# Own places for the decay matrices of a delta rule, and unread products in a matmul engine's gaps

## The chip, the cores and the metric

The kernel runs on one core of one Trainium2 chip. The metric is device time in microseconds of one execution of the whole program. A core has a matmul engine (PE), three engines for elementwise work (DVE, ACT and POOL) and a queue engine (SP) that only issues transfers; each works its own instructions in a fixed order, and semaphores join them. The profile shows for every stretch of time the clock that PE was granted, as a share of full speed.

## The reference

One layer of a diffusion backbone with post-norm, over 512 latent tokens and 256 context tokens of width 1024, all in float32. Cut to what matters here:

```python
# half-step SwiGLU FFN (d_ff 2816) with adaLN shift/scale/gate from c, then in parallel
#   neighbourhood attention (8 heads of 64) and a gated DeltaNet (4 heads of 128, both
#   directions), merged by sigmoid gates, then a second half-step SwiGLU FFN.
def gated_delta_chunks(q, k, v, g, beta, s0, with_output):   # chunks of 64 tokens
    g      = cumsum(g)                                       # within a chunk
    decay  = exp(where(lower, g[..., :, None] - g[..., None, :], -inf))
    m      = where(strict, (k * beta) @ k.T * decay, 0)
    u, w   = solve(eye + m, [v * beta, k * beta * exp(g)])   # unit lower triangular
    # over the chunks: v_new = u - w S;  S = S * exp(g_end) + k_tail.T v_new
    #                  o = (q exp(g)) S + (q @ k.T * decay) v_new

def branch_merge(o_a, o_b, gate_a, gate_b, w_pa, w_pb, w_o):
    y = sigmoid(gate_a) * (o_a @ w_pa) + sigmoid(gate_b) * (o_b @ w_pb)
    return y @ w_o
```

## The kernel before

**Products.** A float32 operand is split into a high part, which ACT casts (`split`, L135), and a low part, which DVE subtracts from the source (L137). Every product of a weight is then three matmuls, high by high, low by high and high by low (`mm3k`, L190 to L192). A weight of 128x1024 comes by DMA into `wr`, is split into `wh` and `wl`, and serves 8 tiles of 128 rows. `uxh` and `uxl` are the parts of the modulated latent tokens, `uch` and `ucl` those of the context tokens.

**Stages.** First come the modulation vectors (`w_ada`, L279 on DVE) with the first FFN's up products (to 213 us), then its down products with the layer norms (to 610 us). Then the projections of `w_in` follow, and with them the delta rule's preparation (to 745 us), the delta rule itself, laid between the rest of those projections (to 993 us), attention in four head pairs with the delta rule's output gates between them (to 1093 us), the merge with `w_pa` (to 1119 us) and `w_o` (to 1140 us). The second FFN begins with up products over half the tokens, goes on with units of seven products (1200 to 1400 us), and ends with its down products and the last norm.

**The delta rule.** It works in three groups of four "grams". A gram is one pair of heads p and one step s, with four 64-token chunk matrices side by side (two heads, two directions; 128x4x128). For each (`gram`, L914) SP loads the row of cumulated decays spread over all partitions into `Dt` (L918, 256 KB, from `gcd`); DVE subtracts the column and adds the mask (L921, four instructions); ACT takes the exponential; DVE multiplies it by the key products into `Bt` (L927, four instructions); SP writes `Bt` to DRAM (`bd`, L928); and where queries are due, DVE multiplies `Dt` with the query products into `At` (L931). `Dt` is a ring of two places: a third load waits until a gram has read its own decays for the last time.

`base_inverse` (L935) reads a group's `bd` back as 32x32 blocks (`L`, `Ltr`, L947), solves all of them by 31 steps of a multiply and a sum on DVE (L954, L955), and writes the result to DRAM (`rd`, L959). `inverse` reads it as `T` (L976), and PE joins the blocks (L857, `pi`). Between these instructions PE works off the rest of the projections (`fills`; their results leave PSUM by ACT into `spill`, L609). While group 0's base inverse runs on DVE, group 1's grams run between its steps; group 0's `inverse` cannot begin before its base inverse has ended.

**Order.** The program is written once, and a planner with a model of each engine's time sets every engine's order. `tc.issue_after(x)` binds an instruction behind instruction `x` in that plan. Tiles come from rings by tag and count, so a tag's next tile waits for the release of the one that many places before.

**Attention.** For a head pair, `att_load` (L1163) brings query, key and context key (`qa`, `ka`, `kc`), ACT casts their high parts (L1169) and POOL subtracts the low parts in place (L1170). `attend` computes scores for four blocks (L1240), exponentials on ACT (L1248), a scaling by the row sum on POOL (L1251), transposes on PE (L1255), the copy of the transposed block to SBUF on ACT (`pT`, L1257) and the products with the values (`po`, L1266).

## Time and profile before

| What | Value |
|---|---|
| Time of three runs | 1526.37, 1526.87 and 1531.96 us; median 1526.87 us |
| The profiled execution | 1530.66 us; its span 1528.8 us |
| Mean granted clock | 0.988 |
| PE busy | 1462.6 us of the span |
| DVE, ACT, POOL busy | 1050.0, 605.4, 226.8 us |

The profiled execution is one of its own, 3.79 us above the median of the three. Its span leaves out 1.86 us that its time has. A row of a timeline gives an instruction's start and length, its engine and line, what it writes and reads, and in square brackets the idle time ahead of it with what ended it; PE's lengths overlap, since matmuls are pipelined, so that the distance from one start to the next is the pace. A row of windows gives each engine's busy time in a stretch, then the granted clock, the DMA share and the rate.

### The profile page before, as it was taken

To read this page: it belongs to the slowest core of one execution; us is meant where nothing else is said; L and a number is where in the kernel's file an instruction comes from. 1 tells how busy PE (TensorE), PEld (TensorE's weight loads), DVE (VectorE), ACT (ScalarE), POOL (GpSimd) and SP (SyncE) were. 2 spreads that over 40 slices of the span, in tenths; PEclk is the share of its full clock that TensorE was granted. 3 is DMA by queue.
4 is the path that set the end of the run, shared out by engine and by line. 5 is a ranking of instruction groups with operands and counts; after the bars stand their busy time and mean duration, and the time that the engine had idled before them with its cause. 6 is when DMAs were issued, how large, how long until landed. Compare 5 with 4: busy or idle time off the path is not lost.

```text
span 1528.8 us, 23646 instructions
## 1 busy us (share of the span) xinstructions
PE 1462.6 (96%) x9221; PEld 1258.7 (82%) x9221; DVE 1050.0 (69%) x1792; ACT 605.4 (40%) x1005; POOL 226.8 (15%) x224
## 2 busy tenths in 40 slices
PE   6999999999999999999996899999999999999997
PEld 4779988888888887889875778867678999998886
DVE  8765942597554587768777895576669699886426
ACT  5444221322222255546543444266416444344310
POOL 0000000000000011323301001366421022220001
PEclk9999999999999999999998999999999999999999
DMA  9665742667454334222476634283353143333422
GB/s 370 207 237 180 222 142 97 211 213 260 168 192 146 130 112 137 87 90 79 141 216 180 172 99 122 69 284 117 91 174 138 56 139 102 106 110 139 138 83 83
DMA packets 107586, 230.72 MB, mean 151 GB/s; under 512 B 34177, under 2 KB 47825, under 8 KB 107473
## 3 DMA queue, kind: packets, MB, share of 16 engines
q1 hardware_dynamic: 105312, 221.79, 44.7%
q10 hardware_dynamic: 1586, 5.32, 0.9%
q0 software_dynamic: 576, 2.10, 0.4%
q8 instruction: 72, 1.18, 0.3%
q14 instruction: 40, 0.33, 0.1%
HBM read 206.33 MB, written 22.85 MB: 150 GB/s over the span
## 4 chain that ended last, share of the span: by engine, by line
PE 76%; DVE 10%; DMA 7%; issue 3%; ACT 2%; POOL 2%; SPq 0%; DVEq 0%; ACTq 0%; POOLq 0%
PE ps L209 19%; PE ps L190 8%; PE ps L192 8%; PE ps L191 8%; PE pm L190 5%; PE pm L192 5%; PE pm L191 5%; PE pc L857 2%; PE ps L1478 2%; PE ps L1480 2%; PE ps L1479 2%; DVE wl L137 2%; PE po L1266 1%; DMA T<-rd 1%; PE pt L1255 1%
## 5 line engine op out<-in xcount | busy, mean ns | idle before, releaser
L137 DVE TENSOR_TENSOR wl<-wr,wh 128x1024 fp32r<-128x1024 f32 (+1 forms) x215 | 263.0, 1228 | 195.1 <-ACT wh L135 194.3
L135 ACT CAST wh<-wr 128x1024 fp32r<-128x1024 f32 (+1 forms) x215 | 217.8, 1018 | 333.4 <-PE ps L209 105.0
L192 PE MATMUL ps<-uxh,wl 128*128 128x512 f32 (+1 forms) x496 | 179.6, 363 | 2.2 <-DVE wl L137 2.2
L191 PE MATMUL ps<-uxl,wh 128*128 128x512 f32 (+1 forms) x496 | 179.3, 363 | 0.8 <-DVE uxl L137 0.8
L190 PE MATMUL ps<-uxh,wh 128*128 128x512 f32 (+1 forms) x496 | 179.6, 365 | 0.0
L279 DVE SCALAR_TENSOR_TENSOR adap<-wr,crow 128x1024 f32<-128x1024 f32 x112 | 136.8, 1221 | 38.5 <-DMA wr<-in_w_adaT_dram 37.1
L112 POOL TENSOR_TENSOR rs<-ve,mhalf 128x1 f32<-128x1 f32 (+2 forms) x46 | 50.4, 1099 | 744.6 <-DVE ve L108 735.4
L190 PE MATMUL pm<-uxh,wh 128*128 128x512 f32 x320 | 133.0, 416 | 4.1 <-ACT spill L609 2.1
L192 PE MATMUL pm<-uxh,wl 128*128 128x512 f32 x320 | 128.2, 401 | 0.7 <-DVE wl L137 0.7
L191 PE MATMUL pm<-uxl,wh 128*128 128x512 f32 x320 | 127.8, 399 | 0.0
L192 PEld LDWEIGHTS ps<-uxh,wl 128*128 128x128 f32 x496 | 93.7, 189 | 17.9 <-DVE wl L137 3.3
L191 PEld LDWEIGHTS ps<-uxl,wh 128*128 128x128 f32 x496 | 94.0, 189 | 14.9 <-DVE uxl L137 1.0
L190 PEld LDWEIGHTS ps<-uxh,wh 128*128 128x128 f32 x496 | 93.4, 189 | 14.3 <-issue 0.8
L190 PE MATMUL ps<-uch,wh 128*128 128x256 f32 x352 | 98.6, 280 | 0.0
L192 PE MATMUL ps<-uch,wl 128*128 128x256 f32 x352 | 98.3, 279 | 0.0
L191 PE MATMUL ps<-ucl,wh 128*128 128x256 f32 x352 | 98.2, 279 | 0.0
L209 PE MATMUL ps<-wh,hx 128*128 128x512 f32 x352 | 94.8, 389 | 0.0
L209 PEld LDWEIGHTS ps<-wh,hx 128*128 128x128 f32 x352 | 65.9, 188 | 13.6
L190 PEld LDWEIGHTS pm<-uxh,wh 128*128 128x128 f32 x320 | 61.6, 193 | 16.3 <-ACT spill L609 3.0
L192 PEld LDWEIGHTS pm<-uxh,wl 128*128 128x128 f32 x320 | 61.7, 193 | 14.8 <-DVE wl L137 1.5
L191 PEld LDWEIGHTS pm<-uxl,wh 128*128 128x128 f32 x320 | 61.6, 192 | 10.6
L190 PEld LDWEIGHTS ps<-uch,wh 128*128 128x128 f32 x352 | 66.1, 188 | 0.6
(411 smaller groups left out, 3438.7 us busy)
## 6 DMA issues: line engine op xcount, KB each, us to landing
wr<-in_w_adaT_dram SPq DMA_DIRECT2D x88, 512.0 KB, 4.7
wr<-in_up_dram SPq DMA_DIRECT2D x80, 512.0 KB, 4.2
wr<-in_dn_dram SPq DMA_DIRECT2D x58, 512.0 KB, 3.5
wr<-in_win_dram SPq DMA_DIRECT2D x52, 512.0 KB, 3.9
rb<-in_up_dram SPq DMA_DIRECT2D x18, 512.0 KB, 3.7
wr<-in_w_o_dram SPq DMA_DIRECT2D x8, 512.0 KB, 4.0
ac<-in_up_dram SPq DMA_DIRECT2D x6, 512.0 KB, 5.2
Dt<-gcd SPq DMA_DIRECT2D x12, 256.0 KB, 5.1
```

What stands on the lines that cost most here:

```text
L112: G.tensor_tensor(rs[:], ve[:], mhalf[:, 0:n], ALU.pow)
L135: S.copy(hi, src)
L137: V.tensor_tensor(lo, src, hi.bitcast(F32), ALU.subtract)
L190: T.matmul(ps, a, uh[:, k, :], start=(k == 0), stop=False)
L191: T.matmul(ps, a, ul[:, k, :], start=False, stop=False)
L192: T.matmul(ps, b, uh[:, k, :], start=False, stop=(k == nk - 1))
L209: T.matmul(banks[t][d][:, c0:c1], a[:, sl], b[:, d * 512 + c0:d * 512 + c1], start=first and j == 0, stop=last and j == 2)
L279: V.scalar_tensor_tensor(pr[:], raw[:], 1.0, crow, op0=ALU.mult, op1=ALU.mult, accum_out=col[:, c:c + 1])
L857: last[0] = T.matmul(*a, **k).ins
L1478: T.matmul(ps[:], a, uh[:, k], start=k == 0, stop=False)
L1479: T.matmul(ps[:], a, ul[:, k], start=False, stop=False)
L1480: T.matmul(ps[:], b, uh[:, k], start=False, stop=k == 3)
```

## The change

It has seven parts. Line numbers are those of the kernel before.

1. At the start a tile is filled with zeros (it is a place of the ring `hc`), and products of it go to an accumulator place that nothing reads (`keep`): 8 behind the spreading of the modulation row, then 10, 5, 0 and 3 behind the transposes of the four token tiles for the first k.
2. Ahead of the transposes of the second context tile after the first FFN, one product of 128x64 goes into a place of the `ps` ring. The places that later tiles get are thereby others.
3. The decays of the delta rule's first two groups get places of their own: the eight grams' `Dt` are two from the ring, four in `oacc0` to `oacc3`, and two more in `oacc0` and `oacc1`. `oacc` is the scan's output sum; it becomes four tiles in place of two and is used by the scans after these grams. The third group uses the ring of two. The subtraction of the decay column (L921) is bound behind the preceding gram's last `Bt` for steps above 3.
4. Ahead of group 0's first `inverse`, 34 products of 128x512 go into a `pc` place that nothing reads.
5. The casts of the next head pair's `qa`, `ka` and `kc` (L1169) are bound behind the `pT` copies of block 0 of the pair in work, from the second pair on.
6. In the merge, the splitting of the sixth `w_o` weight is bound behind that of the last `w_pa` weight loaded by then.
7. In the second FFN's first products, 10 products of 128x256 go into a `ps` place that nothing reads.

```diff
     def split(src, hi, lo, behind=()):
         with tc.issue_after(behind[0]) if behind else nullcontext():
-            S.copy(hi, src)
+            a = S.copy(hi, src).ins
         with tc.issue_after(behind[1]) if behind else nullcontext():
-            V.tensor_tensor(lo, src, hi.bitcast(F32), ALU.subtract)
+            b = V.tensor_tensor(lo, src, hi.bitcast(F32), ALU.subtract).ins
+        return a, b
...
-                split(raw[:, 0:c], hi[:, 0:c], lo[:, 0:c], self.behind.get(self.i, ()))
+                self.last = split(raw[:, 0:c], hi[:, 0:c], lo[:, 0:c], self.behind.get(self.i, ()))
...
+    def keep(n, out, a, b, behind):
+
+        for _ in range(n):
+            with tc.issue_after(behind):
+                T.matmul(out, a, b, start=True, stop=True)
...
-        T.matmul(ps, b, uh[:, k, :], start=False, stop=(k == nk - 1))
+        marks["mm"] = T.matmul(ps, b, uh[:, k, :], start=False, stop=(k == nk - 1)).ins
...
-            T.transpose(ps[:, t * P:(t + 1) * P], x_t[:, k * P:(k + 1) * P], ident)
+            tr = T.transpose(ps[:, t * P:(t + 1) * P], x_t[:, k * P:(k + 1) * P], ident).ins
+            if kind == "x" and k == 0:
+                keep(KEEP[1 + t], wps[:], zero[:, 0:P], zero, tr)
...
+    KEEP = (8, 10, 5, 0, 3)
+    zero = tl(hcp, [P, 2, NCT], "hc", HF, F32R)[:].rearrange("p a n -> p (a n)")
+    G.memset(zero.bitcast(F32), 0.0)
+    wps = tl(pp0, [P, NX], "acc", 2 * F0)
     spread_crow(pp0, crow, 0)
+    keep(KEEP[0], wps[:], zero[:, 0:P], zero, marks["mm"])
...
     u2(fc, pp, "c", 0, ys[0])
     next(units[0])
+
+    keep(1, tl(pp, [P, 512], "ps", 8)[:, 0:64], uxh[:, 0, 0:P], uxh[:, 0, 0:64], marks["mm"])
     u2(fc, pp, "c", 1, ys[1])
...
+    gram_n, bt_last = [0], [None]
+
     def gram(p, s, bd, g):
 
         mats = mats_of(s)
-        Dt = tl(gb_, [P, 4, P], "Dt", 2)
+
+        k = (None, None, 0, 1, 2, 3, 0, 1, None, None, None, None)[gram_n[0]]
+        gram_n[0] += 1
+        Dt = tl(gb_, [P, 4, P], "Dt", 2) if k is None else tl(gq, [P, 4, P], f"oacc{k}")
         nc.sync.dma_start(Dt[:], bass.AP(gcd.tensor, gcd.offset + (4 * s + 2 * p) * P, [[0, P], [24 * P, 2], [1, 2 * P]]))
         for m, (d, c, i) in enumerate(mats):
             msk = cst[:, (C_MF if d == 0 else C_MB):][:, 0:P]
-            V.scalar_tensor_tensor(Dt[:, m], Dt[:, m], gcum[:, d, s, 2 * p + i:2 * p + i + 1], msk, op0=ALU.subtract, op1=ALU.add)
+            with tc.issue_after(bt_last[0]) if s > 3 else nullcontext():
+                V.scalar_tensor_tensor(Dt[:, m], Dt[:, m], gcum[:, d, s, 2 * p + i:2 * p + i + 1], msk, op0=ALU.subtract, op1=ALU.add)
...
-    oaccs = [tl(gq, [P, 4, 2, P], f"oacc{p}") for p in range(2)]
+
+    oaccs = [[], []]
+
+    def out_of(p, c):
+        return oaccs[p][c // 2][:, 2 * (c % 2):2 * (c % 2) + 2]
...
     base = grams(1)
+    keep(34, tl(pgq, [P, 4, P], "pc", 2)[:].rearrange("p m c -> p (m c)"), uxh[:, 0, 0:P], uxh[:, 0, :], marks["mm"])
     inv_of(0, 0)
     step(base, 4)
     inv_of(0, 1)
     step(base)
+    for k in range(4):
+        oaccs[k // 2].append(tl(gq, [P, 4, P], f"oacc{k}"))
...
-    def att_load(p, m):
+    def att_load(p, m, behind=None):
...
-            S.copy(hi[:], lo[:].bitcast(F32))
+            with tc.issue_after(behind) if behind else nullcontext():
+                S.copy(hi[:], lo[:].bitcast(F32))
...
-                S.copy(pT[:], pt[:])
+                turned[b] = S.copy(pT[:], pt[:]).ins
...
-            ready = att_load((na_, ne)[m % 2], m + 1)
+
+            ready = att_load((na_, ne)[m % 2], m + 1, turned[0] if m else None)
...
         gt, ps = gated("pa", gad, m, oah, oal)
+        if m == 2:
+
+            wso.behind[5] = ws.last
...
             ffn_unit(lp, pp, *w0[f], uxh[:, :, sl], uxl[:, :, sl], 256, h[0][:, sl], h[1][:, sl])
+            if i == 0 and f == NH - 1:
+                keep(10, tl(pp, [P, 256], "ps", 8)[:], w0[f][0][0][:, 0:P], uxh[:, 0, sl], marks["mm"])
```

The planner sets the order anew, and three places show what moves. The first is SP's queue at the delta rule's beginning, where `Dt` is a decay load, `bd` the write of a gram's `Bt`, `Ltr` and `L` the blocks read back, `qad`, `kad`, `vad` and `gad` stores of projections, and `wr` a weight of the fills. Before:

```order
L918 DMA Dt_6802<-gcd_4994 128x2x256
L918 DMA Dt_6839<-gcd_4994 128x2x256
...
L928 DMA bd_1221_6800<-Bt_6809 128x4x128
L918 DMA Dt_6867<-gcd_4994 128x2x256
L928 DMA bd_1221_6800<-Bt_6846 128x4x128
L918 DMA Dt_6904<-gcd_4994 128x2x256
L613 DMA vad_4993<-spill_6864 128x512
L172 DMA wr_7110<-in_win_dram 128x1024
L928 DMA bd_1221_6800<-Bt_6874 128x4x128
L918 DMA Dt_7045<-gcd_4994 128x2x256
L928 DMA bd_1221_6800<-Bt_6911 128x4x128
L918 DMA Dt_7135<-gcd_4994 128x2x256
```

And now (the lines of this function are 21 or 22 higher):

```order
L939 DMA oacc_1234_6896<-gcd_5023 128x2x256
L939 DMA oacc_1241_6933<-gcd_5023 128x2x256
L627 DMA qad_5020<-spill_6792 128x512
L939 DMA oacc_1280_7074<-gcd_5023 128x2x256
L939 DMA oacc_1296_7164<-gcd_5023 128x2x256
L627 DMA kad_5021<-spill_6826 128x512
L173 DMA wr_7095<-in_win_dram 128x1024
L950 DMA bd_1222_6829<-Bt_6838 128x4x128
L939 DMA Dt_8003<-gcd_5023 128x2x256
L950 DMA bd_1222_6829<-Bt_6875 128x4x128
L939 DMA Dt_8030<-gcd_5023 128x2x256
```

The loads of grams 2 to 5 (`oacc`) now stand ahead of the first `bd` write and behind no gram; the two loads behind the first two `bd` writes are already those of the third group (`Dt_8003`, `Dt_8030`).

The second place is DVE at the same stretch (`wl` are low parts of the fills' weights, `At` the query product times the decays, `bt` the base inverse's first step). Before, from the decays of group 0's third gram to the first step of the base inverse:

```order
L921 SCALAR_TENSOR_TENSOR Dt_6867<-Dt_6867,gcum_5005,cst_5002 128x128 x4
L137 TENSOR_TENSOR wl_6888<-wr_6885,wh_6887 128x1024
L921 SCALAR_TENSOR_TENSOR Dt_6904<-Dt_6904,gcum_5005,cst_5002 128x128 x4
L927 SCALAR_TENSOR_TENSOR Bt_6874<-pq_6875,beta_5004,Dt_6867 128x128 x4
L927 SCALAR_TENSOR_TENSOR Bt_6911<-pq_6875,beta_5004,Dt_6904 128x128 x4
L137 TENSOR_TENSOR wl_7069<-wr_7066,wh_7068 128x1024
L921 SCALAR_TENSOR_TENSOR Dt_7045<-Dt_7045,gcum_5005,cst_5002 128x128 x4
L921 SCALAR_TENSOR_TENSOR Dt_7135<-Dt_7135,gcum_5005,cst_5002 128x128 x4
L927 SCALAR_TENSOR_TENSOR Bt_7052<-pq_7053,beta_5004,Dt_7045 128x128 x4
L954 TENSOR_TENSOR bt_6946<-L_6932,Xt_6934 128x2
```

And now, from the decays of the same gram on, with group 0's first two `Bt` behind them:

```order
L943 SCALAR_TENSOR_TENSOR oacc_1280_7074<-oacc_1280_7074,gcum_5034,cst_5031 128x128 x4
L943 SCALAR_TENSOR_TENSOR oacc_1296_7164<-oacc_1296_7164,gcum_5034,cst_5031 128x128 x4
L949 SCALAR_TENSOR_TENSOR Bt_6903<-pq_6904,beta_5033,oacc_1234_6896 128x128 x4
L137 TENSOR_TENSOR wl_6917<-wr_6914,wh_6916 128x1024
L949 SCALAR_TENSOR_TENSOR Bt_6940<-pq_6904,beta_5033,oacc_1241_6933 128x128 x4
L943 SCALAR_TENSOR_TENSOR oacc_1313_7263<-oacc_1313_7263,gcum_5034,cst_5031 128x128 x4
L137 TENSOR_TENSOR wl_7098<-wr_7095,wh_7097 128x1024
L943 SCALAR_TENSOR_TENSOR oacc_1330_7362<-oacc_1330_7362,gcum_5034,cst_5031 128x128 x4
L949 SCALAR_TENSOR_TENSOR Bt_7081<-pq_7082,beta_5033,oacc_1280_7074 128x128 x4
L953 TENSOR_TENSOR At_7128<-pq_7120,oacc_1280_7074 128x512
L976 TENSOR_TENSOR bt_6975<-L_6961,Xt_6963 128x2
```

The decays of all four grams of group 1 are now subtracted ahead of the base inverse (`oacc_1280` to `oacc_1330`), where two of them stood in it; those of group 0's last two grams (not in the rows) stand ahead of its first `Bt`.

The third place is ACT in attention (`pr` are the exponentials, `pT` the transposed block's copy, `oah` and `wh` casts for the gates, and the casts of L1169 those for the fourth head pair). Before, with the `pT` copies of the second head pair's block 0 around them:

```order
L1248 ACTIVATE pr_9809,sm_9810<-sc_9771,nm_9807 128x512 x2
L135 CAST wh_9898<-wr_9896 128x512
L135 CAST oah_9360<-oa_9592 128x512
L1257 COPY pT_9741<-pt_9736 128x512
L1169 CAST kah_10227<-ka_10228 128x512
L1169 CAST qah_10222<-qa_10223 128x512
L135 CAST wh_10054<-wr_10052 128x512
L1169 CAST kch_10232<-kc_10233 128x256
L1257 COPY pT_9748<-pt_9743 128x512
```

And now, with the `pT` copies of the third head pair's block 0 ahead of them:

```order
L1287 COPY pT_10077<-pt_10072 128x512
L135 CAST oah_9428<-oa_10018 128x512
L135 CAST wh_10346<-wr_10344 128x512
L1287 COPY pT_10084<-pt_10079 128x512
L1278 ACTIVATE pr_10190,sm_10191<-sc_10174,nm_10188 128x512 x2
L1197 CAST qah_10290<-qa_10291 128x512
L1197 CAST kah_10295<-ka_10296 128x512
L1197 CAST kch_10300<-kc_10301 128x256
```

The fourth pair's casts have moved a whole pair back, and they stand no more between two `pT` copies. The third pair's now stand in the second half of the second pair.

On PE the 34 products stand as one row of 34 behind the last product of the fills and ahead of group 0's first `pi` product; the one product of 128x64 stands ahead of the second context tile's transposes.

## The prediction

> **What bounds the kernel now.** I read the page's busy shares and its chain first, then the granted clock in windows, and then PE's waits stage by stage.

> ```profile
> PE 1462.6 (96%) x9221; PEld 1258.7 (82%) x9221; DVE 1050.0 (69%) x1792; ACT 605.4 (40%) x1005; POOL 226.8 (15%) x224
> PE 76%; DVE 10%; DMA 7%; issue 3%; ACT 2%; POOL 2%; SPq 0%; DVEq 0%; ACTq 0%; POOLq 0%
> ```

> PE sets the end. It idles 1528.8 − 1462.6 = 66.2 us. That is all that could be won by waits alone; to it comes the time that PE works at half clock after a gap, which counts as busy. The change removes no product; it can win only in these two. So I went through the gaps where its parts stand.

> **The ring place (part 2).** The timeline at the first FFN's end, PE's rows and then the ACT row that it waited for, and the window behind:

> ```profile
> 607.60 1.03 PE L146 MATMUL ps<-ident,y 128*128 128x128 f32 x8
> 610.56 0.58 PE L190 MATMUL pm<-uxh,wh 128*128 128x512 f32 x1 [1.92 <-ACT u L149]
> 614.31 0.39 PE L190 MATMUL pm<-uxh,wh 128*128 128x512 f32 x1
> 614.54 0.39 PE L191 MATMUL pm<-uxl,wh 128*128 128x512 f32 x1
> ```

> ```profile
> 609.00 2.90 ACT L149 ACTIVATE u<-ps,colc 128x128 f32<-128x128 f32 x8
> ```

> ```profile
> 612.00:614.00 2.00, 2.00 (x6) 1.52 (x6) 1.46 (x3) 1.98 (x4) 0.00 (x0) 0.50 0.30 123
> ```

> The product at 610.56 reads `uxh` and a weight that had long been there; it waits only because its PSUM tile takes the place that ACT is still reading. The transposes go to another place with the change, so it can start behind them: −1.9 us. Then the clock, granted at 0.50 behind the wait, stays up as well: nine products stand from 610.56 to 614.31, 3.75 us (0.42 each), where nine at the full pace (614.31 to 614.54, 0.23) take 2.1, so −1.6. PE's next waits are in the delta rule, so both are kept at least until there. The extra product of 64 columns costs under 0.23. Bounds: −1.5 (ACT's copies become the next wait, since the other tile holds transposes too) to −3.6; I take −3.4.

> **The decays (part 3) and the 34 products (part 4).** DVE's waits in 745 to 820 us, and its timeline through group 0's base inverse:

> ```profile
> DVE Dt L921 <- DMA Dt<-gcd: 12.7, 6, 5.0
> ```

> ```profile
> 760.22 1.14 DVE L921 SCALAR_TENSOR_TENSOR Dt<-Dt,gcum,cst 128x128 f32<-128x128 f32 x4 [4.95 <-DMA Dt<-gcd]
> 769.21 1.14 DVE L921 SCALAR_TENSOR_TENSOR Dt<-Dt,gcum,cst 128x128 f32<-128x128 f32 x4 [2.46 <-DMA Dt<-gcd]
> 776.25 0.16 DVE L954 TENSOR_TENSOR bt<-L,Xt 128x2 f32<-128x2 f32 x1 [3.36 <-POOL L L950]
> 783.28 0.88 DVE L921 SCALAR_TENSOR_TENSOR Dt<-Dt,gcum,cst 128x128 f32<-128x128 f32 x3 [3.00 <-DMA Dt<-gcd]
> 794.74 1.14 DVE L921 SCALAR_TENSOR_TENSOR Dt<-Dt,gcum,cst 128x128 f32<-128x128 f32 x4 [1.11 <-DMA Dt<-gcd]
> 807.59 1.14 DVE L921 SCALAR_TENSOR_TENSOR Dt<-Dt,gcum,cst 128x128 f32<-128x128 f32 x4 [0.77 <-DMA Dt<-gcd]
> 817.40 0.69 DVE L955 TENSOR_REDUCE Xt<-bt 128x16 f32<-128x512 f32 x1
> ```

> The inverse runs from 776.25 to 818.1. In it stand 3.00 + 1.11 + 0.77 = 4.9 us of waiting for `Dt`, and ahead of it 4.95 + 2.46 and a small one. These loads come late because the third to eighth wait for a ring place. On SP and PE, and PE's waits in 770 to 840 us:

> ```profile
> 765.64 0.45 SPq L928 DMA_DIRECT2D bd<-Bt  x1
> 820.06 4.31 SPq L959 DMA_DIRECT2D rd<-Xt  x4
> 826.42 2.02 SPq L976 DMA_DIRECT2D T<-rd  x4
> ```

> ```profile
> 786.72 0.50 PE L190 MATMUL pm<-uxh,wh 128*128 128x512 f32 x1 [1.53 <-ACT spill L609]
> 788.77 0.63 PE L192 MATMUL pm<-uxh,wl 128*128 128x512 f32 x1
> 812.20 1.05 PE L857 MATMUL pq<-qT,kT 128*128 128x128 f32 x8
> 818.32 0.39 PE L192 MATMUL pm<-uxh,wl 128*128 128x512 f32 x1
> 831.15 0.68 PE L857 MATMUL pi<-T,Bt 32*32 32x32 f32 x32 [12.44 <-DMA T<-rd]
> ```

> ```profile
> PE pm L190 <- ACT spill L609: 2.1, 2, 1.5
> PE pm L192 <- DVE wl L137: 0.7, 2, 0.3
> ```

> PE has worked off its fills at 818.7 and stands still for 12.44 us: the inverse's end, the write of `rd`, its reading as `T`. The end at 818.1 sets this gap's end; whatever the inverse gains is gained one for one, as long as the transfers behind it take the same 13.05 us (818.1 to 831.15).

> With own places, group 0's last `Bt` no longer waits for the ring, and the write at 765.64 stands some 4 us earlier, at most by the 4.95 of its wait; the inverse then begins near 772.4. In it the three waits and two of the three decay subtractions (1.1 each) go: 41.85 − 4.9 − 2.2 = 34.8, so DVE alone could end at 807. But the last gram needs PE's query product (812.20), behind fills that PE works without pause. PE's own waits before it (2.1 + 0.7 = 2.8) and the half clock behind the one at 786.72 (the product at 788.77 is 0.63 long, not 0.39; priced as the nine at 610.56, 1.6) are what it can gain: some 4.5 us, so the product comes near 808 and the inverse ends near 810. That is −8 (818.1 to 810); the bounds are −5.7 (the later end of the gram's product chain, with the added `Dt` of group 2's first gram late in the inverse) and −8.2 (all). The six loads, moved ahead, are 256 KB each on SP's queue ahead of the projections' stores and of a weight load: an issue of some 0.45 as the write beside them, for four of them 1.8 us of delay for a weight of the fills; I take this as hidden by the fill's weights in hand, and as +1.8 if not. The load ring for the third group has as many places as before.

> The 34 products run at 0.23 us, 7.7 us together, in a gap that still begins with PE's last fill and now is 9 to 11 us long, since PE also ends its fills 4.5 us earlier. They end 1 to 3 us ahead of `T`, and delay nothing. What they may win is the clock behind the gap:

> ```profile
> 822.50:825.00 2.50, 0.00 (x0) 0.00 (x0) 1.73 (x8) 0.63 (x1) 0.15 (x1) 0.50 0.66 109
> 832.50:835.00 2.50, 2.50 (x34) 1.56 (x36) 2.33 (x9) 1.00 (x2) 2.30 (x5) 0.50 0.28 89
> ```

> From 831.15 to about 836 PE is at half clock, worth up to 2 us; DVE is 2.33 of 2.5 busy there, though, and takes some of it. I take −1 of 0 to −2, and −6 for the inverse, within its bounds but below my own −8 since the next inverse inherits a full DVE: −7 together (−3 to −10).

> How much idleness drops the clock matters here. In this trace the one wait of 1.53 us at 786.72 is followed by half clock (788.77). [...]

> **The casts in attention (part 5).** ACT's rows between the pairs, POOL's, and PE's:

> ```profile
> 1032.25 0.62 ACT L1169 CAST kah<-ka 128x512 fp32r<-128x512 f32 x1 [4.01 <-DMA ka<-kad]
> 1034.25 0.58 ACT L1257 COPY pT<-pt 128x512 f32<-128x512 f32 x1
> ```

> ```profile
> 1032.95 1.27 POOL L1170 TENSOR_TENSOR ka<-ka,kah 128x512 fp32r<-128x512 f32 x1 [5.12 <-DMA qa<-qad]
> 1036.61 3.10 POOL L1251 TENSOR_SCALAR pr<-pr,sm 128x512 f32<-128x512 f32 x2
> ```

> ```profile
> 1034.88 0.90 PE L1266 MATMUL po<-pT,vw 128*64 128x128 f32 x5 [1.88 <-ACT pT L1257]
> ```

> ```profile
> 1030.00:1040.00 10.00, 7.33 (x49) 5.71 (x48) 3.33 (x6) 5.69 (x14) 6.74 (x5) 0.70 0.54 191
> ```

> ACT stands 4.01 us for a load, ahead of a copy that PE needs; PE idles 10 − 7.33 = 2.7 us in this window, and has a mean clock of 0.70, so some 3 us of it are lost to the half clock. The bound casts stand behind the copies. Gain: −2 (the wait alone) to −5 (clock too). But the planner orders the whole stage anew, and the casts, with POOL's subtractions behind them, come later for their own pair; what that costs no row shows. Bounds −6 to +3; I take −3.

> **The smaller parts.** In the merge, and in the second FFN's beginning:

> ```profile
> PE pm L192 <- DVE wl L137: 2.7, 2, 1.8
> ```

> ```profile
> 1194.52 0.98 PE L190 MATMUL ps<-uxh,wh 128*128 128x256 f32 x7
> 1195.35 0.28 PE L191 MATMUL ps<-uxl,wh 128*128 128x256 f32 x1
> 1195.46 0.28 PE L192 MATMUL ps<-uxh,wl 128*128 128x256 f32 x1
> ```

> Binding the `w_o` split leaves DVE free for the low part that PE awaits, 2.7 us in all; DVE's next work may be late as well: −0.5 (−2 to +1.5). The 10 products take 10 × 0.12 = 1.2 us at 1194.5, where PE worked seven products ahead and had only 0.8 us to spare: +0.7 (+0.4 to +0.9). At the start:

> ```profile
> 27.76 0.19 PEld L414 LDWEIGHTS acc<-uxl,wh 128*128 128x128 f32 x1 [0.41 <-DVE uxl L137]
> L279 DVE SCALAR_TENSOR_TENSOR adap<-wr,crow 128x1024 f32<-128x1024 f32 x112 | 136.8, 1221 | 38.5 <-DMA wr<-in_w_adaT_dram 37.1
> ```

> A warmer clock there brings PE sooner to data that are not there: the stage goes by loads (37.1 us of DVE's idle time waits for them). I take 0 (−1.5 to +0.5). The seven-product units' order changes a little too: 0 (±2, as wide as the merge's).

> **The sum.** −3.4 − 7 − 3 − 0.5 + 0.7 = −13.2. The profiled execution, 1530.66, would be 1517.5; it lies 3.79 above the median, so against the median 1526.87 the change gives 1513.7, near 1514.

> **The rivals.** *(a) The later stages take it back.* The gain of 3.4 and 7 is at hand at 831, but PE is fed by loads and DVE in the scans (DVE 2.3 of 2.5 busy behind 832) and by loads in attention, and what comes sooner waits there. Only the first wait and 2 to 3 us of the rest last: −3.4 − 2 = −5.4, 1521.5. For it speaks the full DVE; against it PE's 96%. *(b) Slower: the bound casts come too late.* They wait for the `pT` copies, POOL's three subtractions stand behind a pair of `pr` scalings (3.10), and the next pair's scores wait for them: 3.1 + 3.7 (three subtractions by 1032.95 to 1036.61) + 1.7 for the clock, 8.5 us per pair, twice: +17 for −3, so −10.2 + 17 = +6.8, 1533.7. It decides from the point where POOL ends its last subtraction behind PE's last product of the pair ahead. Against it: the rows now put them half a pair ahead or more, and POOL has 3 of 10 us free (6.74 busy). *(c) The 34 products run at half clock*, 0.42 each, 14.3 us: from 814.2 they end at 828.5, after `T` has come, and of the −7 only 2.6 are left: 1518. Against it: PE comes into the gap at full clock.
> [...]

> **How the numbers follow.** Forecast 0.60 (likeliest alone 1507 to 1521), (a) 0.18, (b) 0.10, (c) 0.12. A measurement tells about 0.5%, 7.6 us, from no change: faster is below 1519.2, slower above 1534.5. Faster: 0.95 of the forecast, half of (c), a sixth of (a): 0.57 + 0.06 + 0.03 = 0.66. Slower: 0.06 of (b) and 0.03 for an order in the units that I misread: 0.09. Same: 0.25. The range goes from 1504, the forecast with most terms at their good ends, to 1528, which holds (a) and (c) and leaves (b) out.

> **What would show it.** In the changed kernel's profile the first `pm` product starts within 0.3 us of the transposes, with the clock at 1.00 in the windows behind; DVE waits for no `Dt` until group 2; the inverse ends 6 to 8 us sooner against its stage's beginning; PE's idle time ahead of the first `pi` is under 4 us; ACT's wait for `ka` is away from the `pT` copies. Wrong would be a `T` that comes no sooner, a `pi` row waiting on PE's own 34 products, PE rows that wait for POOL's `qa` or `ka`, or a new wait of the fills for `wl`.

## The result: 9 us slower, and the profile after

The changed kernel takes 1537.62 us (median of 9 runs, 1532.70 to 1541.36), the kernel before 1528.32 (1526.37 to 1531.96). The ratio is 1.0054, with a 95% interval of 1.0036 to 1.0072: slower by half a percent, where I had forecast 1514. The difference is 9.3 us by the medians and 8.2 by the ratio. The profiled execution of the change has a span of 1535.5 us, 6.7 above that of before.

I set each PE instruction of the one profile against the same instruction of the other. The table gives how much later it starts (negative: sooner), and so where the time went in this pair of profiles. Where the two orders differ, at attention's beginning above all, the figure is rough.

| From (us in before) | Change minus before | What lies there |
|---|---|---|
| 20 to 57 | −0.05 | the start, with the zero products |
| 60 | +8.9 | second spreading of the modulation row |
| 110 to 600 | +6.1 | first FFN: 2.8 made good by loads |
| 620 | +2.6 | behind the ring place: −3.5 |
| 830 to 855 | −2.5 to −3.7 | behind the first inverse: −5 to −6 |
| 880 to 990 | +2.2 to +3.4 | scans: +6 |
| 1005 to 1025 | +5 to +10 | attention's beginning, in another order |
| 1045 | +4.2 | behind the casts: −2 to −5 |
| 1070 to 1100 | +7 | third head pair: +3 |
| 1120 | +9.3 | merge: +2 |
| 1200 to the end | +6.8 | second FFN |

The start came as a surprise. PE's row of before there, then PE's rows of the change, and the windows around them:

```profile
57.37 1.98 PE L290 MATMUL ps<-crow,one_row 1*128 1x512 f32 x4
```

```profile
57.01 0.39 PE L429 MATMUL acc<-uxh,hx 128*128 128x512 f32 x1
61.97 3.77 PE L297 MATMUL ps<-crow,one_row 1*128 1x512 f32 x4 [4.57 <-DVE fs L279]
65.67 0.80 PE L197 MATMUL ps<-uxh,wh 128*128 128x512 f32 x1
```

```profile
60.00:65.00 5.00, 3.03 (x4) 1.16 (x4) 2.26 (x4) 2.05 (x4) 0.00 (x0) 0.59 0.51 199
65.00:70.00 5.00, 5.00 (x11) 3.46 (x11) 3.56 (x7) 0.60 (x1) 0.00 (x0) 0.50 0.26 75
```

In before the four small products of the modulation row follow at 57.37 without a wait. Now PE waits 4.57 us for DVE's work on the first FFN tiles, and the clock is at half for 10 us, from 60.9 to 71.2. Nothing that the products multiply is late: the instruction waited for, which writes `fs`, is the last reader of an accumulator.

The ring place did what was forecast. The first `pm` product stands right behind the transposes (PE's timeline):

```profile
613.69 0.19 PE L193 MATMUL ps<-uxh 128*128 128x64 f32 x1
613.72 1.07 PE L147 MATMUL ps<-ident,y 128*128 128x128 f32 x8
614.54 0.48 PE L197 MATMUL pm<-uxh,wh 128*128 128x512 f32 x1
```

At the first inverse, PE's timeline and DVE's:

```profile
820.96 7.87 PE L193 MATMUL pc<-uxh 128*128 128x512 f32 x34
828.75 0.45 PE L873 MATMUL pi<-T,Bt 32*32 32x32 f32 x32
829.14 0.50 PE L197 MATMUL pm<-uxh,wh 128*128 128x512 f32 x1
```

```profile
756.33 2.40 DVE L943 SCALAR_TENSOR_TENSOR oacc<-oacc,gcum,cst 128x128 f32<-128x128 f32 x8 [5.39 <-DMA oacc<-gcd]
771.94 1.14 DVE L943 SCALAR_TENSOR_TENSOR oacc<-oacc,gcum,cst 128x128 f32<-128x128 f32 x4 [4.70 <-DMA oacc<-gcd]
780.92 0.69 DVE L953 TENSOR_TENSOR At<-pq,oacc 128x512 f32<-128x512 f32 x1 [3.87 <-ACT kq L917]
```

The gap is filled to its end, and the products behind it run at the full pace (0.34 and then 0.23 us apart). But DVE still waits for decays, counting the grams from 0. It waits 5.39 us for those of grams 2 and 3, which the new order puts ahead of group 0's first `Bt`, and 4.70 us for those of grams 6 and 7, whose places are `oacc0` and `oacc1` for the second time. Then it waits 3.87 us for `kq`, in a product that the new order puts ahead of the first step of the base inverse. That step comes at 781.71, in before at 776.25; this stage as a whole begins 2.6 us later than in before.

In attention, ACT's and PE's rows of the change:

```profile
1013.27 1.32 ACT L1207 COPY vst<-va 128x256 f32<-128x256 f32 x4 [2.22 <-DMA va<-vad]
```

```profile
1016.51 0.48 PE L1270 MATMUL sc<-kah,qah 64*128 64x256 f32 x2 [2.70 <-ACT pr L1278]
1066.81 0.43 PE L1296 MATMUL po<-pT,vw 128*64 128x128 f32 x2 [1.80 <-ACT pT L1287]
```

ACT's wait for `ka` at 1032 us is gone. In its place stands, 20 us sooner, one for `va`, ahead of an exponential (`pr`) that PE needs; and the third pair has a wait of 1.80.

### The profile page after: what moved, and what is told of

Read it like the earlier page. It is cut to its first block, busy times and chain, and to the rows that moved or that the text cites. A ratio compares the mean times of both kernels' runs of the same rounds, so it can differ in the third digit from the quotient of the medians.

```text
span 1535.5 us, 23784 instructions
## 1 busy us (share of the span) xinstructions
PE 1482.6 (97%) x9292; PEld 1276.6 (83%) x9292; DVE 1052.0 (69%) x1792; ACT 606.8 (40%) x1005; POOL 228.3 (15%) x225
## 4 chain that ended last, share of the span: by engine, by line
PE 81%; DVE 9%; DMA 5%; issue 2%; ACT 2%; POOL 1%; SPq 0%; DVEq 0%; ACTq 0%; POOLq 0%
PE ps L216 22%; PE ps L197 9%; PE ps L199 9%; PE ps L198 9%; PE pm L197 5%; PE pm L199 5%; PE pm L198 4%; PE ps L1514 3%; PE ps L1515 3%; PE ps L1516 3%; PE pc L873 2%; DVE wl L137 1%; PE po L1296 1%; PE pt L1285 1%; DMA L<-bd 1%
## 5 line engine op out<-in xcount | busy, mean ns | idle before, releaser
L137 DVE TENSOR_TENSOR wl<-wr,wh 128x1024 fp32r<-128x1024 f32 (+1 forms) x215 | 262.5, 1226 | 197.3 <-ACT wh L135 196.7
```

Source lines behind the costliest of these rows:

```text
L137: b = V.tensor_tensor(lo, src, hi.bitcast(F32), ALU.subtract).ins
```

## The experiments

The runs were taken in four sets, each with runs of the kernel before on the same chip, whose median was 1526 to 1528 us. Kernels of different sets are compared by their ratios to it; 0.001 of a ratio is 1.5 us. Parts are numbered as in the change.

**The start: without part 1.**

```diff
-    wps = tl(pp0, [P, NX], "acc", 2 * F0)
     spread_crow(pp0, crow, 0)
-    keep(KEEP[0], wps[:], zero[:, 0:P], zero, marks["mm"])
...
-            if kind == "x" and k == 0:
-                keep(KEEP[1 + t], wps[:], zero[:, 0:P], zero, tr)
```

> The change without its first part: no zero tile, no products of it, no accumulator place taken at the start; parts 2 to 7 as they are, and no other instruction in another order. Theory A (the place taken ahead of the ring of ps moves the next pool's first tiles onto places whose last readers, DVE's work on the first up products, end late): PE's 4.57 us wait ahead of the second spreading of the modulation row goes, the half clock from 60.9 to 71.2 us with it, and PE is 6 us earlier at 110 us; about 1531.5 us, ratio to before 1.002. Rival B (the loss of the start is made good later, because loads and DVE set the pace from 60 to 100 us anyway): about 1537, ratio 1.005.

Measured: 1530.24 us, ratio 1.0028 (1.0012 to 1.0044). Against the change that is 4 us by the two ratios (7.4 by the medians, but the change's set had the slowest runs of before). It agrees with theory A, whose number was 1531.5.

**One product in the same place.** `KEEP = (1, 0, 0, 0, 0)`.

> The change with one product of zeros at the start where it has 26, into the same accumulator place. Theory A (the place): the wait of 4.57 us and the half clock behind it stay as they are, about 1537.5 us, ratio to before 1.005. Rival C (the 25 other products delay the transposes or upset the clock): about 1531.5 us, ratio 1.002. The products also warm the clock from 10 us on; if that were worth something, this kernel would be slower than the change by up to 1.5 us.

Measured: 1535.64 us, ratio 1.0060 (1.0036 to 1.0083), in the same set as the kernel without part 1 and 5.4 us above it. The wait is there, 4.57 us long, with one product as with 26:

```profile
62.07 3.78 PE L297 MATMUL ps<-crow,one_row 1*128 1x512 f32 x4 [4.57 <-DVE fs L279]
```

**All products, but the places as before.**

```diff
-    wps = tl(pp0, [P, NX], "acc", 2 * F0)
     spread_crow(pp0, crow, 0)
-    keep(KEEP[0], wps[:], zero[:, 0:P], zero, marks["mm"])
+    for _ in range(2 * F0):
+        wps = tl(pp0, [P, NX], "acc", 2 * F0)
+        keep(1, wps[:], zero[:, 0:P], zero, marks["mm"])
+    keep(KEEP[0] - 6, wps[:], zero[:, 0:P], zero, marks["mm"])
```

> The change with its 26 products of zeros at the start, but the accumulator places are asked for behind the ps ring's first tile and all six of that ring are gone through once (a product in each), so that every later tile has the place that it has in the kernel before. Theory A: as without the first part, about 1531.5 us, ratio 1.002, with the clock full from about 10 us on and no 4.57 us wait at 57 us. Rival C (the products): as the change, about 1537.5 us, ratio 1.005. If the warm clock at the start is worth anything, this one beats the kernel without the first part by up to 1.5 us.

Measured: 1531.34 us, ratio 1.0026 (1.0009 to 1.0043), the same as without the products. The small products start at 57.32 without a wait:

```profile
57.32 1.98 PE L297 MATMUL ps<-crow,one_row 1*128 1x512 f32 x4
59.23 0.50 PE L197 MATMUL ps<-uxh,wh 128*128 128x512 f32 x1
```

So it is the place. `wps` is asked for before the first `ps` tile of its pool, and the addresses in the two programs show what follows. The first pools of the two programs take eight places of PSUM, 0 to 7. In before, and with the places cycled as here, the `ps` ring has places 0 and 1 and the accumulators the other six; in the change the accumulators have 0 to 5 and the ring 6 and 7. The next pool's first tile takes place 0 in all of them. That was a place of the ring, long free; in the change it is the place of the last accumulator, which DVE reads until 61.91. The tile of zeros, too, takes a place (in the ring `hc`); it does so in the cycled kernel as well, and costs nothing there. The products themselves, and a clock that is at full 14 us sooner (from 11.5 us in this kernel, from 25.2 without part 1), bring nothing.

**Without the 34 products, and the 34 alone** (part 4 undone; part 4 alone in the kernel before).

```diff
-    keep(34, tl(pgq, [P, 4, P], "pc", 2)[:].rearrange("p m c -> p (m c)"), uxh[:, 0, 0:P], uxh[:, 0, :], marks["mm"])
```

> The change without the 34 products ahead of group 0's first inverse (the planner then lays attention's first value copies, vst, behind the exponentials of the third block as in the kernel before; scans and attention are planned anew). Theory D (the planner counts the 34 products, and the order it then makes sets ACT waiting 2.22 us for the load va ahead of an exponential that PE needs; 2.70 us of waiting and two spells of half clock, about 6 us at 1000 us): that wait goes; at 831 us the half clock behind the gap comes back, at most 2 us; about 1533.5 us, ratio 1.0035. Rival E (what is lost at 860 and at 1000 us is a matter of where the clock's drops fall and not of order): no gain at 1000 us, 1 to 2 us lost at 831, about 1539 us, ratio 1.007.

> The kernel before with part 4 alone, the 34 products ahead of the first inverse, in a gap that is 12.44 us long there. Theory D (the planner's order of attention's beginning follows from its counting these products): the clock is held or lost only for the last 4 us of the gap, −2 to 0 at 836 us; ACT waits for va ahead of an exponential at 1000 us, +6: ratio 1.002 to 1.004. Rival E (that order is harmless by itself): −2 to 0, ratio 0.999 to 1.0.

Measured: 1535.58 us, ratio 1.0055 (1.0038 to 1.0073), without them; 1532.60, ratio 1.0049 (1.0024 to 1.0074), with them alone. Alone they do harm, and theory D names a good part of it. ACT's and PE's rows of the kernel with them alone, at attention's beginning and at the first inverse:

```profile
1013.80 1.32 ACT L1194 COPY vst<-va 128x256 f32<-128x256 f32 x4 [3.70 <-DMA va<-vad]
```

```profile
1017.04 0.58 PE L1257 MATMUL sc<-kah,qah 64*128 64x256 f32 x2 [5.16 <-ACT pr L1265]
```

```profile
816.99 7.87 PE L193 MATMUL pc<-uxh 128*128 128x512 f32 x34
833.09 0.68 PE L865 MATMUL pi<-T,Bt 32*32 32x32 f32 x32 [8.22 <-DMA T<-rd]
```

The order now has the copies of `va` ahead of the exponentials, and the load is 3.7 us late; as I read it, the planner counts 7.9 us more of PE ahead of attention and expects `va` to be there by then, which no run shows by itself. And the 34 products end 8.22 us before `T`, and the clock falls all the same: PE's products from 834.29 to 836.00 us start 0.43 us apart, those from 837.61 us on 0.23. Against the second profile of before (below), this kernel loses some 5 us at attention's beginning and 4 more in the scans, between 870 and 900 us; the latter stays unexplained.

In the change, their removal costs the clock behind the gap (6.8 us of half clock from 824.4) and saves the wait for `va`, and the two cancel: the ratios are 1.0055 and 1.0054. The wait for `va` goes, as theory D had it; the time, for which D had 1533.5 and rival E 1539, decides for neither.

**Parts 2, 3 and 5; part 3 alone; part 5 alone.** All three from the kernel before, with the lines of the change's diff for these parts.

> The kernel before with three parts alone: the product into a ps place after the first FFN (2), the places for the decays (3) and the bound casts in attention (5). No products at the start, none ahead of the first inverse, none in the second FFN, no bound w_o split. Theory D (each part's gain is its own, and parts 1 and 4 cost 6 us each): −3.5 at 615 us, −5 at 825, of which some 4 are given back by 880 (the next inverse's chain), no new wait at 1000 us since the value copies stand behind the exponentials, −5 at 1035, +3 in the third head pair: about −6.5, 1521.5 us, ratio 0.996. Rival E (the losses at 880 and 1000 us come from PE being early there, whatever the order, and eat every gain): within 2 us of before, ratio 0.999 to 1.001.

> The kernel before with part 3 alone, the places for the decays. Theory A (the first inverse gains 5 us, the second inverse's chain of DVE steps, rd writes and T reads is next and gives back 4): −5 at 830 us, −1 from 880 on, ratio 0.999 to 1.0. Rival F (the gain lasts): −5 at the end, ratio 0.997.

> The kernel before with part 5 alone, the bound casts in attention. Theory G (they take away the 4.01 us wait of ACT and the half clock behind it, −5 at 1040 us, and make PE wait 1.8 us for a pT copy in the third pair, with half clock behind it, +3): −2, ratio 0.998 to 0.999. Rival H (the third pair's wait comes from other parts): −5, ratio 0.997.

Measured: 1529.95 us, ratio 1.0037 (1.0020 to 1.0053); 1534.76, ratio 1.0062 (1.0044 to 1.0080); 1529.12, ratio 1.0025 (1.0007 to 1.0043). All of my theories fall here: the decays by themselves are not 1 us faster but 8 slower (four runs). Against the second profile of before, PE gains 8 us at the first inverse and gives 7 back in the scans, as theory A had it in kind; then it loses 5 us in attention and 5 in the merge, which no theory of mine had. PE's rows in the merge, of the kernel with the decays alone and of the one with the casts alone:

```profile
1105.48 0.79 PE L197 MATMUL pm<-oah,wh 128*128 128x512 f32 x1 [3.03 <-ACT wh L135]
1108.72 0.79 PE L199 MATMUL pm<-oah,wl 128*128 128x512 f32 x1 [1.17 <-DVE wl L137]
```

```profile
1098.81 0.50 PE L197 MATMUL pm<-oah,wh 128*128 128x512 f32 x1 [2.89 <-ACT wh L135]
```

No such wait stands in before. In both kernels the new order has ACT cast three `w_o` weights of 128x1024 ahead of the `w_pa` weights of 128x512 that PE needs; in before there are two. Part 6 binds one of these casts.

**The rest alone: parts 2, 6 and 7, and the kernel before profiled again.**

> The kernel before with part 2 alone, the one product into a ps place after the first FFN; no other instruction moves. Theory A (the place): PE no longer waits 1.92 us for ACT ahead of the first pm product at 610 us and, where the clock fell behind that wait, it stays up; between −1.9 (clock unharmed in the kernel before) and −3.5 us at 620 us, kept to the end: about 1523.5 us, ratio 0.9975 to 0.999. Rival E (what is gained ahead of the delta rule is lost in its chains and in attention): ratio 0.9995 to 1.001.

> The kernel before with part 6 alone, the bound w_o split in the merge. Theory M (DVE splits the w_pa weights sooner, PE waits less than the 2.7 us of before): −1 us, ratio 0.999 to 1.0. Rival N (the order that the planner makes then lays low parts of y and of other weights ahead of the one that PE needs; 2 us of waiting in one piece, which can bring half clock): +1 to +3, ratio 1.0005 to 1.002.

> The kernel before with part 7 alone, the 10 products of 128x256 in the second FFN's beginning. Theory O (they fill a wait of 0.8 us and cost the rest of their 1.2): +0.4, ratio 1.000 to 1.0005. Rival P (they keep the clock up at 1190 us, where it falls behind the 2.14 us wait ahead of them): −1.7, ratio 0.999.

> The kernel before, unchanged, profiled a second time. Theory K (the clock falls on a grid of 3.41 us whose beginning differs from run to run, at the end of a stretch of it in which PE was busy for less than about half): the waits of 1.7 to 3.4 us stand where they stood (1.92 at 610 us, 1.53 at 787, 2.80 at 864, 1.88 at 1035, 2.14 at 1186, and those of the merge), but other ones of them are followed by half clock; the gap of 12.44 us is followed by it in every run. Rival L (the drops belong to places of the program): the same drops as in the first profile. Ratio 1.000.

Measured: part 2 1525.35 us, ratio 0.9990 (0.9978 to 1.0003), unclear by itself; part 6 1522.52, ratio 0.9965 (0.9947 to 0.9984), faster by a third of a percent; part 7 1527.15, ratio 0.9995 (0.9982 to 1.0008), nothing; before again 1527.46, ratio 0.9997 (0.9983 to 1.0011). What the second profile of before says of theories K and L stands in the last section.

Neither M nor N tells why part 6 gains: in the merge PE waits no less (2.03 us at 1110). Part of it is in the units of the second FFN, whose order follows. PE's waits in 1200 to 1400 us, of the kernel before, profiled again, and of part 6 alone:

```profile
PE ps L1480 <- DVE sl L137: 1.2, 1, 1.2
PE ps L1478 <- DVE sn L1499: 0.9, 1, 0.9
PE ps L1478 <- DVE sn L1502: 0.8, 2, 0.6
```

```profile
PE ps L1500 <- DVE sl L137: 1.2, 1, 1.2
PE ps L1498 <- ACT sh L135: 0.2, 1, 0.2
PE ps L1498 <- DVE sn L1522: 0.2, 1, 0.2
```

Some 1.8 us of waiting for `sn` is gone; where the other 3 us come from stays open.

**Decays with the bound `w_o` split, and with the ring place** (parts 3 and 6; 2 and 6; 2, 3 and 6; 2, 3, 5, 6 and 7).

> The kernel before with parts 3 and 6, the places for the decays and the bound w_o split. Theory Q (most of what the decays by themselves lose is lost in the merge, by a third w_o cast that the planner lays ahead of the w_pa casts): the 3.03 us wait of PE for ACT's cast at 1105 us and the half clock behind it go, −5.2, and part 6 keeps what it gains by itself in the units (−3): about 1526.5 us, ratio 0.998 to 1.001. Rival R (the decays' loss is in scans and attention): about 1531, ratio 1.002 to 1.004.

> The kernel before with parts 2 and 6, the ring place after the first FFN and the bound w_o split. If the two gains add up (−1.5 and −4.5 by their own runs): about 1521, ratio 0.996. If the ring place's gain is lost in the delta rule's chains: as part 6 alone, ratio 0.9965 to 0.998.

> The kernel before with parts 2, 3 and 6. Theory Q: 1.5 to 2 us ahead of the kernel with parts 3 and 6, about 1525 us, ratio 0.997 to 1.0. Rival R: about 1530, ratio 1.002.

> The change without its products of zeros at the start and without the 34 products: parts 2, 3, 5, 6 and 7. Theory D with Q (the place at the start and the order that the 34 products bring are the two large losses, the rest gains a little): 1524 to 1527 us, ratio 0.998 to 1.0. Rival E (attention and scans lose what the decays gain in any order): about 1530 us, ratio 1.002.

| Parts | Median, us | Ratio (interval) |
|---|---|---|
| 3 | 1534.76 | 1.0062 (1.0044 to 1.0080) |
| 3, 6 | 1529.20 | 1.0020 (1.0007 to 1.0033) |
| 2, 6 | 1522.08 | 0.9969 (0.9955 to 0.9983) |
| 2, 3, 6 | 1525.31 | 0.9997 (0.9985 to 1.0010) |
| 2, 3, 5, 6, 7 | 1530.55 | 1.0026 (1.0011 to 1.0040) |

Theory Q has one place right: with the split bound, PE's wait of 3.03 us in the merge is 0.5 us, and the decays lose some 6 us less. It does not have all: part 6 without the decays is 8 us faster than with them, and 2 with 6 is 4.3 us faster than 2, 3 and 6 (by the ratios, as all that follows). The ring place adds nothing that can be told to part 6 (0.9969 against 0.9965), but 3.5 us to parts 3 and 6. The kernel with parts 2 and 6 beats both kernels, before by 4.7 us and the change by 13. Parts 5 and 7 on top of 2, 3 and 6 cost 4.4 us. So the kernel with all but the start and the 34 products is slower than before, as rival E had it (1530): with the start out, the rest of the change still sums to a loss.

What the decays do is seen best in the pair that differs by them alone (2 and 6; 2, 3 and 6). PE's waits for `T` from 740 to 855 us, first without and then with them, and from 855 to 990 with them:

```profile
PE pi L866 <- DMA T<-rd: 15.8, 1, 15.8
```

```profile
PE pi L866 <- DMA T<-rd: 8.1, 1, 8.1
```

```profile
PE pi L866 <- DMA T<-rd: 3.9, 2, 2.1
```

| | Without the decays (2, 6) | With (2, 3, 6) | Difference |
|---|---|---|---|
| First inverse on DVE, first sum to last | 773.85 to 814.57 | 774.74 to 810.38 | end −4.2 |
| Its `T` transposed from | 828.93 | 821.30 | −7.6 |
| Second inverse | 822.38 to 870.95 | 814.62 to 865.70 | end −5.3 |
| Its `T` transposed from | 879.62 | 875.65 | −4.0 |
| Third inverse | 875.91 to 920.23 | 870.26 to 918.11 | end −2.1 |
| Its `T` transposed from | 926.03 | 923.96 | −2.1 |

The gain of the first inverse is handed on and shrinks: 7.6, 4.0, 2.1 us. PE by contrast has its fills and runs 8 us early at 855; so it now waits for the second and third `T` (2.14 and 1.71 us), where it did not. Behind the third wait the clock is at half for 6.8 us, from 932.9; without the decays it is at full there. At 940 us nothing of the 8 is left. Attention, newly ordered, then adds waits of its own (2.51 us for `pT`, 0.83 for `vw` at 1033 us) and 2.6 us of loss.

## Why the prediction was wrong

**Where it failed.** Five of the kernels form a chain: each has the parts of the one above it and one or two more. Their ratios to the kernel before price every step in the company in which the change has it. A step is uncertain by some 3 us (from the intervals of the two ratios). The parts do not simply add up: alone, some of them measure otherwise.

| Step | Forecast, us | Ratio, from and to | Measured, us |
|---|---|---|---|
| Parts 2 and 6 (ring place, `w_o`) | −3.9 | 1 to 0.9969 | −4.7 |
| Part 3 (decays) | −6 | 0.9969 to 0.9997 | +4.3 |
| Parts 5 and 7 (casts, 10 products) | −2.3 | 0.9997 to 1.0026 | +4.4 |
| Part 4 (34 products) | −1 | 1.0026 to 1.0028 | +0.3 |
| Part 1 (start) | 0 | 1.0028 to 1.0054 | +4.0 |
| All | −13.2 | 1 to 1.0054 | +8.2 |

Three terms failed, each with the wrong sign or a nothing that was something: the decays (by 10 us), the casts (by 7) and the start (by 4). None of them alone accounts for the miss. The first row is right by luck: part 2 was given −3.4 and measures −1.5 alone, part 6 was given −0.5 and measures −4.7.

**The start.** "A warmer clock there brings PE sooner to data that are not there [...] I take 0 (−1.5 to +0.5)". The warm clock is indeed worth nothing (the products' removal and their move to other places give the same time). But the step weighed only the products. The place that they write was put at nothing without a reason, though part 2 rests on that very mechanism: a tile taken moves all later ones. It costs 4.0 us by the ratios and 5.4 within one set of runs; in the profile PE is 6.1 us later from 110 us on.

**The decays.** The step "the write at 765.64 stands some 4 us earlier [...] the inverse then begins near 772.4" is wrong. In the change that write stands at 767.27, only 1.0 us sooner if the stage's 2.6 are taken off: the new order has DVE wait 5.39 us for the decays of grams 2 and 3 ahead of group 0's first `Bt`. The second turn of `oacc0` and `oacc1` waits again (4.70 us), and the inverse begins no sooner (774.74 against 773.85 in the pair above). That "the three waits and two of the three decay subtractions (1.1 each) go" is right as a sum: the inverse is 5.1 us shorter (40.72 to 35.63). PE resumes 7.6 us sooner in that pair, within −5.7 to −8.2, but by luck: the inverse's end gives 4.2 of it, and the rest is transfers that happened to be faster, which I had held constant at 13.05 (from the inverse's end to `T` 14.4 us became 10.9; over the kernels it goes from some 10 to 15). That "whatever the inverse gains is gained one for one" holds for that gap alone: I kept the −6 to the end of the kernel, and the scans take it back by 940 us. Rival (a), which I gave 0.18, is what follows, and it goes on: nothing is left, and attention and merge add a loss.

**The planner.** I had costed the new order of attention, merge and units at nothing with some width. The waits that it brings are shown: 5.16 us for the 34 products alone, 3.03 and 2.89 for decays and casts alone. Each of the three parts is harmful by itself in good part through an order far behind its place; part 6 takes one such loss away. Why the planner chose these orders is not shown.

**The casts.** The gain of "−2 (the wait alone) to −5 (clock too)" holds at its place: ACT's wait for `ka` is gone, and PE gains 2 to 5 us there. It is lost in the third head pair, where PE waits 1.80 us for a `pT` copy at 1066 and 3.4 us of half clock follow, from 1067.8, and, with the casts alone, in the merge. Alone the casts are 0.25% slower (1.0007 to 1.0043); on top of parts 2, 3 and 6, with part 7, they cost 4.4 us net. That pair of profiles shows 5 us won at the place, 4 lost in the third pair and 3 more at 1190, where the 10 products stand; the rest stays open. Rival (b) foresaw the sign, not the mechanism: in the change PE waits nowhere in attention for POOL's subtractions.

**The clock.** I priced half clock from one profile as if it belonged to its places: 1.6 us at 610, 1.6 at 788, most of the 3 in attention. In the second profile of the same kernel none of the three is there. The ring place is worth its wait of 1.9 by PE's rows, not 3.4; its own runs (0.9990, 0.9978 to 1.0003) agree with that, and with nothing too. For the 34 products the clock was held in the change, as forecast: it is 1.00 from 788.0 to 859.6 us, and they end where `T` comes (the first `pi` product follows at 828.75 without a wait). In the kernel without part 1 they end 2.70 us before it, and 3.4 us of half clock follow, from 823.9 (as the prediction's row of 1.53 us had warned). Rival (c) was the wrong worry, for the order that the products brought cost what they won.

**The small parts.** Part 7 is nothing that can be told apart (forecast +0.7). Part 6 is mis-sized, and not for the reason named: PE waits no less for the `w_pa` low parts.

## What to carry to other kernels

A tile that is taken to be written and never read is not free: look where every later tile of the pool, and of the pool that takes its room, then lies, and who reads there last. Where a planner sets the order, a local gain has to be looked for at the end of the program, and every part run by itself and in a chain; its losses here stood 70 to 350 us behind the edit. Before a half clock is counted as a gain, see whether a second profile of the same kernel shows it.

## What the runs showed of the hardware

```profile
607.42:610.83 3.41, 1.49 (x11) 1.16 (x10) 1.25 (x2) 3.26 (x8) 0.00 (x0) 1.00 0.01 5
610.83:614.25 3.42, 3.42 (x9) 2.66 (x9) 1.71 (x3) 3.40 (x8) 0.00 (x0) 0.50 0.48 153
```

```profile
608.55:611.96 3.41, 1.87 (x8) 1.57 (x9) 0.86 (x1) 3.41 (x11) 0.00 (x0) 1.00 0.42 137
611.96:615.37 3.41, 3.41 (x17) 2.83 (x16) 3.28 (x5) 2.39 (x4) 0.00 (x0) 1.00 0.07 22
```

Both hold the wait of 1.92 us ahead of the first `pm` product. Where it falls whole into a stretch, PE is busy for 1.49 of 3.41 (44%), and half clock follows; where the grid's edge cuts it, PE is busy for 1.87 (55%), and it does not. Over all profiles, of the stretches at full clock from 30 us on to 12 us before the end, half clock followed on all 49 that were busy for less than 40%, on 34 of 45 between 40 and 50%, on 14 of 61 between 50 and 60%, on 1 of 85 between 60 and 70%, and never on the 194 between 70 and 85%; above that, in the three cases told below alone. In the first profile of before and that of the change taken together, these counts are 6 of 6, 8 of 9, 1 of 4, 0 of 6, 0 of 22, and above that 0 of 803. The full clock came back only behind a stretch that was at least 84% busy (96% in these two profiles). Half clock followed on a stretch that the wait touches for 26 of 50 waits of 1.7 to 2.05 us (5 of 8 in these two), for 25 of 39 of 2.05 to 3 us (4 of 5), and for all 22 above 3 us (2 of 2). Waits of 1.0 to 1.3 us were followed by it too, for 1 of 4 in before and 2 of 5 in the change, where two waits stand in one stretch: 0.59 and 1.12 us in before (at 935.8 and 937.4, PE busy for 1.70 of 3.41), 1.29 and 1.17 us in the change (at 939.0 and 940.6, busy for 1.39). The wait of 2.80 us at 864 in before was not followed by half clock in the first profile, and was in the second.

The times agree with it: over 111 runs of the kernel before in the four sets, the mean granted clock goes from 0.985 to 0.993, and the runs with less of it tend to be the slower ones (correlation of time with half-clock time 0.65). It explains a part of why one kernel's runs lie between 1519.8 and 1533.2 us, and why a few us in one profile are no finding.

In the three cases above 85%, four products of a single row stand whole in the stretch. In the kernel with the casts alone, PE counts as busy for all 3.41 us of it, the 1.98 of these products among them, and half clock follows (timeline, then windows):

```profile
57.45 1.98 PE L297 MATMUL ps<-crow,one_row 1*128 1x512 f32 x4
```

```profile
56.59:60.00 3.41, 3.41 (x12) 1.64 (x11) 3.41 (x5) 2.03 (x4) 0.00 (x0) 1.00 0.65 179
60.00:63.40 3.40, 3.40 (x10) 2.65 (x9) 2.37 (x4) 2.29 (x5) 0.00 (x0) 0.51 0.71 286
```

In 15 of the 18 profiles these four products run without a wait. They fall whole into one stretch of the grid in four of them, and half clock follows in three of the four; in the other eleven an edge cuts them, and it never follows. No run isolates what these products do to the clock.
